# An encoder layer on one core: V projected in its own stretch and passed through DRAM, and one operand fewer fetched before the down phase

## The chip, the cores and the metric

The kernel runs on one core of a Trainium2 chip. The metric is the device time of one execution in microseconds (us). Before the change the median of three runs is 1965.58 us (1962.38 to 1968.96).

## The reference, cut to what matters

One layer of 1024 tokens and width 1024 in float32: a SwiGLU feed-forward block, a mixer of two attention kinds, and a second SwiGLU block, each followed by a residual sum and a layer norm. All of V comes out of the same product as Q and K, `p = h @ w_in`.

```python
def hybrid_mixer(h, w_in, w_out, ...):
    p = h @ w_in
    na_q, na_k, na_v, df_q, df_k, df_v = jnp.split(p, splits, axis=-1)
    na_out = neighbourhood_attention(na_q, na_k, na_v, na_rpb)   # 8 heads of 64, window 8 x 16
    df_out = differential_attention(df_q, df_k, df_v, ...)       # 4 heads, q and k of 2 x 64, v of 128
    return jnp.concatenate([na_out, df_out], axis=-1) @ w_out

x = layer_norm(a * x + 0.5 * swiglu(x, ffn1...))
x = layer_norm(a * x + hybrid_mixer(x, ...))
x = layer_norm(a * x + 0.5 * swiglu(x, ffn2...))
```

## The kernel before, in words

Each large product is made of three matmuls per term: both operands are split into a rounded part and a remainder (`split`: a cast on ScalarE, then a subtraction on VectorE or GpSimd), and hi x hi, hi x lo and lo x hi are added up in PSUM (`mm3`). A matmul is 128 x 128 against 128 x 512 columns wherever it can be.

The stages, in order: `gate_up` and `down_phase` of the first block, the attention, the product with w_out, `gate_up` and `down_phase` of the second block. All transfers are issued by the SP queue, in order. The order of the instructions on each engine is fixed when the program is built, by a scheduler that starts from the order of the code; the engines then run their lists in order and wait on semaphores.

**Attention.** There are eight groups: four differential heads (DF), then four pairs of neighbourhood heads (NA). `project(g)` makes K, V and Q of a group for both halves of the tokens, 24 matmuls for each of K, V and Q in each half. Its output has features as rows, so V has to be turned: `df_v` and `na_v` do it with transposes on TensorE (16 blocks of 128 x 128 per NA group, 8 per DF group), followed by copies. The projection of the first group runs alone. The other seven are fillers: `project` is a generator, cut into 48 pieces of three matmuls, and `Filler` places two pieces at each of 24 places of the attention of the group ahead. One DF group has eight units (blocks of 128 queries). A unit is: scores on TensorE, a sum with a minimum on VectorE (`df_scores`, L682), an exponential on ScalarE (L685), the reciprocal and the combination of the two maps on VectorE (L687 to L689), transposes of the result (L697), its split (L699, L700), and for every second unit the product with V (`df_out`, L706). An NA group has eight shorter units (`na_scores`, `na_transpose`, `na_out`); the last NA group has no filler.

**Down phase.** `fetch_down` loads a pair of operands (half of it activations from `hSd`, half weights), and splits it into a buffer of the pool `wsp` (4 buffers) or `hd`. `gate_up` fetches the operands 0 to 3 ahead, through the two staging buffers of the pool `wst`, which the last activations (`hPd`) also pass through. `down_phase` fetches the others through a pool of its own with six buffers.

Of the kernel before, what the change touches and what calls it, by code (L numbers as in the profile page):

```python
# [9 lines left out]
FT = mybir.dt.float32  # L10
# [11 lines left out]
P = 128  # L22
# [15 lines left out]
NA_R = [(0, 11), (4, 12)]  # L38
NA_C = [(0, 24, 0), (8, 32, 1), (24, 32, 1), (40, 24, 2)]
NA_KINDS = [(24, 0), (32, -8), (24, -8)]  # L40
NA_VOFF = [0, 16 * 24, 16 * 56, 16 * 88, 16 * 112]
RAW = 14 * NCOL + 32


# [1 line left out]
def tile_hybrid_layer(ctx: ExitStack, tc: tile.TileContext, I: dict, out: bass.AP, dbg=None):  # L46
# [22 lines left out]
    def split_w(src, pool=wsp, tag="wsp", eng=G):  # L69
        st = wst.tile([P, 1024], FT, name="wst")  # L70
        dma(st, src)
        sp = pool.tile([P, 2, 1024], FR, name=tag)
        split(sp[:, 0], sp[:, 1], st, eng)
        return sp
# [20 lines left out]
    x1d = dr.tile([8, P, DM], FT, name="x1d")  # L95
    x2d = dr.tile([8, P, DM], FT, name="x2d")
    oTd = dr.tile([8, P, S], FT, name="oTd")

    hPd = [dr.tile([4, P, S], FT, name=f"hPd{i}") for i in range(2)]
    hSd = [[dr.tile([P, 7, 512], FT, name=f"hSd{i}_{p}") for p in range(NP)] for i in range(2)]  # L100
# [107 lines left out]
    def gate_up(n, wgu, wd, W0=None, prelude=None):  # L208


        with ExitStack() as es:
# [152 lines left out]
            for f in range(2, NF):  # L364
# [37 lines left out]
                    sum_down(p)  # L402
                elif p + 1 < NP:
                    load_down(p + 1)
            down0.append(fetch_down(n, wd, 3, wst, wsp, "wsp"))
        return down0

    def down_phase(es, n, wd, down0, resid, g, b, post):
# [132 lines left out]
    def nothing():  # L541
        return
        yield

    with ExitStack() as es:
        kp = es.enter_context(tc.tile_pool(name="kp", bufs=2))
        qp = es.enter_context(tc.tile_pool(name="qp", bufs=3))
        vtp = es.enter_context(tc.tile_pool(name="vtp", bufs=1))
        sm = es.enter_context(tc.tile_pool(name="sm", bufs=6))
        mp = es.enter_context(tc.tile_pool(name="mp", bufs=1))  # L550
        rp = es.enter_context(tc.tile_pool(name="rp", bufs=2))
# [1 line left out]
        def project(g):  # L553

            h, na = g["h"], g["kind"] == "na"
            cq, ck, cv = (h, 4 + h, 8 + h) if na else (12 + h, 16 + h, 20 + h)
            scale = -0.125 if na else -0.125 / SLOPES[h]
            wk, wv, wq = (split_w(I["w_in"][c]) for c in (ck, cv, cq))
            K = g["K"] = kp.tile([P, 2, S], FR, name="K")
            VT = g["VT"] = vtp.tile([P, NA_VOFF[4] if na else S], FT, name="VT")  # L560
            g["Q"] = []

            def mm(w, t):
                ps = psB.tile([P, 512], FT, name="psB")
                for k in range(KT):
                    hi, lo = w[:, 0, k * P:(k + 1) * P], w[:, 1, k * P:(k + 1) * P]
                    xh, xl = xk(t, k)
                    T.matmul(ps, hi, xh, start=k == 0, stop=False)  # L568
                    T.matmul(ps, hi, xl, start=False, stop=False)  # L569
                    T.matmul(ps, lo, xh, start=False, stop=k == KT - 1)  # L570
                    if k < KT - 1:
                        yield ps
                yield ps

            for t in range(2):
                ts = slice(t * 512, (t + 1) * 512)
                for ps in mm(wk, t):
                    yield
                for j in range(2):
                    a, b = slice(64 * j, 64 * j + 64), slice(64 - 64 * j, 128 - 64 * j)  # L580
                    A.activation(K[a, j, ts], ps[a], AF.Copy, scale=scale)
                    V.scalar_tensor_tensor(K[b, j, ts], ps[a], scale, K[a, j, ts].bitcast(FT), OP.mult, OP.subtract)
                for ps in mm(wv, t):
                    yield
                if na:
                    psg = ps.rearrange("p (r c) -> p r c", c=GW)
                    for c, (c0, nc_, _) in enumerate(NA_C):
                        o = NA_VOFF[c] + 8 * t * nc_
                        A.copy(VT[:, o:o + 8 * nc_].rearrange("p (r c) -> p r c", c=nc_), psg[:, :, c0:c0 + nc_])
                else:  # L590
                    A.copy(VT[:, ts], ps)
                flush()
                Q = qp.tile([P, 2, 2, 512], FR, name="Q")
                g["Q"].append(Q)
                for ps in mm(wq, t):
                    yield
                for j in range(2):
                    a, b = slice(64 * j, 64 * j + 64), slice(64 - 64 * j, 128 - 64 * j)
                    qi, hi, lo = ps[a], Q[a, j, 0], Q[a, j, 1]
                    if na:  # L600
                        qi = qi.rearrange("p (r c w) -> p c r w", c=4, w=16)
                        hi, lo = (x.rearrange("p (c r w) -> p c r w", c=4, w=16) for x in (hi, lo))
                    A.copy(hi, qi)
                    V.tensor_tensor(lo, qi, hi.bitcast(FT), OP.subtract)
                    dma(Q[b, j].bitcast(FT), Q[a, j].bitcast(FT))

        PIECES = 48
        groups = [dict(kind="df", h=h) for h in range(4)] + [dict(kind="na", h=h) for h in range(4)]

        def filler(i, places):  # L610
# [35 lines left out]


        with ExitStack() as e2:
            vp = e2.enter_context(tc.tile_pool(name="vp", bufs=1))
            ep = e2.enter_context(tc.tile_pool(name="ep", bufs=3))  # L650
            ap = e2.enter_context(tc.tile_pool(name="ap", bufs=2))
            dp = e2.enter_context(tc.tile_pool(name="dp", bufs=1))
# [1 line left out]
            dist = dp.tile([P, 1920], FH, name="dist")  # L654
            dma(dist, I["dist"])

            def df_v(g):
                Vt = g["V"] = vp.tile([P, 2, KT, P], FR, name="Vt")
                for c in range(2):
                    ps = psB.tile([P, 4, P], FT, name="psB")  # L660
                    for k in range(4):
                        o = (4 * c + k) * P
                        T.transpose(ps[:, k], g["VT"][:, o:o + P], ident)
                    hi = Vt[:, 0, 4 * c:4 * c + 4]
                    A.copy(hi, ps)
                    V.tensor_tensor(Vt[:, 1, 4 * c:4 * c + 4], ps, hi.bitcast(FT), OP.subtract)

            def df_scores(g, qb):
                slope = SLOPES[g["h"]]
# [80 lines left out]
            for i, (g, qb) in enumerate(units):  # L750
                if qb == 0 and i:
                    fill.drain()
                    fill = filler(i // 8 + 1, 24)
                queue.append((g, qb, df_scores(g, qb)))
                if tail:
                    tail.pop()()
                fill()
                if qb == 1:
                    df_v(g)
                if len(queue) > 1:  # L760
                    df_rest()
            fill.drain()
# [10 lines left out]
        with ExitStack() as e2:  # L773
# [21 lines left out]
                        o += n * nc_  # L795

            def na_v(g, c):
                nc_ = NA_C[c][1]
                Vc = vp.tile([P, 4, P], FT, name="Vc")
                ps = psB.tile([P, 4, P], FT, name="psB")  # L800
                for k in range(4):
                    o = NA_VOFF[c] + 4 * k * nc_
                    T.transpose(ps[0:4 * nc_, k], g["VT"][:, o:o + 4 * nc_], ident)
                V.tensor_copy(Vc[0:4 * nc_], ps[0:4 * nc_])
                return Vc

            def na_scores(g, r, c, tabs):
# [157 lines left out]
def _layout(inp):  # L965
# [11 lines left out]
    for i in (1, 2):  # L977
        r[f"wgu{i}"] = gu(a[f"ffn{i}_w_gate"], a[f"ffn{i}_w_up"])
        r[f"wd{i}"] = a[f"ffn{i}_w_down"].reshape(NF, P, DM)
    r["w_in"] = np.ascontiguousarray(  # L980
        a["w_in"][0].reshape(KT, P, 24, P).transpose(2, 1, 0, 3)).reshape(24, P, KT * P)
    r["w_out"] = a["w_out"].reshape(8, P, DM)
    r["rpb"] = np.pad(a["na_rpb"].reshape(-1)[::-1], (RPB_PAD, RPB_PAD))
    for n in ("lq1", "lk1", "lq2", "lk2"):
# [36 lines left out]
```

## Time and profile before

| | before |
|---|---|
| median of three runs | 1965.58 us |
| profiled execution: its time / its span | 1969.43 us / 1967.7 us |
| TensorE (PE) busy | 1926.4 us, 98%, 9152 matmuls |
| VectorE (DVE) busy | 1217.6 us, 62% |
| ScalarE (ACT) busy | 762.3 us, 39% |
| GpSimd (POOL) busy | 208.8 us, 11% |
| mean granted TensorE clock | 0.993 |
| HBM read / written | 183.42 MB / 72.88 MB |

The span runs from the first to the last instruction; the time of the execution has some 2 us around it. Busy time of TensorE is the sum of the durations of pipelined matmuls, which overlap; how many matmuls a stretch really takes is read from their starts.

### The profile page before, as it was taken

The numbers are of one execution on the slowest core, as the hardware profiler recorded it, in microseconds if no ns is written. First come the engines' busy times: TensorE is split into PE (matmuls) and PEld (weight loads), VectorE is DVE, ScalarE is ACT, GpSimd is POOL, SyncE is SP. The second block draws the span as 40 slices with busy tenths as digits, with TensorE's granted clock in tenths as the row PEclk, the third lists the DMA queues.
The fourth block names the chain that finished last, engine by engine and source line by source line (L and its number), as shares of the span: only waits on it lengthen the run. The fifth ranks groups of instructions, "written<-read, shape, count | busy, mean of one in ns | idle before, by whom it ended". The sixth has DMA issues, their size and how long they took to land.

```text
span 1967.7 us, 24088 instructions
## 1 busy us (share of the span) xinstructions
PE 1926.4 (98%) x9152; PEld 1562.2 (79%) x9152; DVE 1217.6 (62%) x1823; ACT 762.3 (39%) x1228; POOL 208.8 (11%) x188
## 2 busy tenths in 40 slices
PE   9999999999999999999999999999999999999998
PEld 7777887877887878888777777887787888878887
DVE  8575655545555956778663346787666646455557
ACT  5333333334333245556544455133333333344331
POOL 0000000000001312011044443100000000000005
PEclk9999999999999999999999999999999999999999
DMA  4556323248762331112122226224555222387632
GB/s 168 208 203 222 120 102 118 102 166 300 235 196 88 106 91 41 49 41 62 30 56 67 64 65 226 83 89 160 192 205 191 93 102 99 125 294 254 195 119 86
DMA packets 90771, 266.26 MB, mean 135 GB/s; under 512 B 11680, under 2 KB 15648, under 8 KB 82976
## 3 DMA queue, kind: packets, MB, share of 16 engines
q1 hardware_dynamic: 90656, 264.73, 39.3%
q8 instruction: 72, 1.18, 0.2%
q14 instruction: 43, 0.35, 0.1%
HBM read 183.42 MB, written 72.88 MB: 130 GB/s over the span
## 4 chain that ended last, share of the span: by engine, by line
PE 42%; DMA 3%; DVE 3%; ACT 1%; issue 1%; POOL 0%; SPq 0%; POOLq 0%; DVEq 0%; ACTq 0%
PE psA L80 5%; PE psA L82 5%; PE psA L81 5%; PE psA L435 5%; PE psB L435 4%; PE psB L80 3%; PE psB L81 3%; PE psB L82 3%; PE psB L568 2%; PE psB L570 2%; PE psB L569 2%; PE psB L851 2%; PE psA L818 1%; DMA wr<-in_wgu 1%; PE psB L843 1%
## 5 line engine op out<-in xcount | busy, mean ns | idle before, releaser
L80 PE MATMUL psA<-x,wsp 128*128 128x512 f32 x448 | 181.5, 405 | 8.8 <-ACT t L377 5.3
L80 PE MATMUL psA<-s,wsp 128*128 128x512 f32 x480 | 189.6, 395 | 0.0
L82 PE MATMUL psA<-s,wsp 128*128 128x512 f32 x480 | 187.4, 390 | 0.0
L81 PE MATMUL psA<-s,wsp 128*128 128x512 f32 x480 | 186.7, 389 | 0.0
L66 ACT CAST wsp<-wr 128x1024 fp32r<-128x1024 f32 x124 | 128.9, 1049 | 128.9 <-DVE wr L205 121.3
L81 PE MATMUL psA<-x,wsp 128*128 128x512 f32 x448 | 175.8, 392 | 0.5 <-DVE x L67 0.5
L82 PE MATMUL psA<-x,wsp 128*128 128x512 f32 x448 | 175.1, 391 | 0.0
L568 PE MATMUL psB<-x,wsp 128*128 128x512 f32 x384 | 160.5, 418 | 0.0
L67 DVE TENSOR_TENSOR wsp<-wr,wsp 128x1024 fp32r<-128x1024 f32 x124 | 149.5, 1223 | 12.9 <-ACT wsp L66 12.9
L570 PE MATMUL psB<-x,wsp 128*128 128x512 f32 x384 | 152.2, 396 | 0.0
L569 PE MATMUL psB<-x,wsp 128*128 128x512 f32 x384 | 150.9, 393 | 0.0
L67 POOL TENSOR_TENSOR wsp<-wst,wsp 128x1024 fp32r<-128x1024 f32 x28 | 67.6, 2415 | 759.3 <-ACT wsp L66 759.3
L67 DVE TENSOR_TENSOR hd<-wst,hd 128x1024 fp32r<-128x1024 f32 x84 | 102.0, 1223 | 73.0 <-ACT hd L66 68.2
L204 DVE TENSOR_TENSOR wr<-wr 128x1024 f32<-128x1024 f32 x40 | 49.0, 1225 | 148.6 <-DMA wr<-in_wgu 148.6
L66 ACT CAST hd<-wst 128x1024 fp32r<-128x1024 f32 x84 | 87.7, 1054 | 124.7 <-PE psA L435 36.3
L66 ACT CAST wsp<-wst 128x1024 fp32r<-128x1024 f32 (+1 forms) x90 | 93.0, 1034 | 105.5 <-DMA wst<-in_wd 27.9
L67 DVE TENSOR_TENSOR wsp<-wst,wsp 128x1024 fp32r<-128x1024 f32 (+1 forms) x62 | 73.8, 1190 | 84.1 <-ACT wsp L66 76.0
L80 PEld LDWEIGHTS psA<-x,wsp 128*128 128x128 f32 x448 | 84.1, 188 | 45.4 <-ACT t L377 16.1
L435 PE MATMUL psA<-hd 128*128 128x512 f32 x504 | 116.2, 389 | 0.0
L144 POOL TENSOR_TENSOR mv<-mv,cols 128x1 f32<-128x1 f32 x24 | 35.5, 1478 | 721.1 <-DVE mv L143 721.1
L435 PEld LDWEIGHTS psA<-hd 128*128 128x128 f32 x504 | 94.6, 188 | 19.7
L80 PEld LDWEIGHTS psA<-s,wsp 128*128 128x128 f32 x480 | 90.0, 188 | 25.4 <-ACT sg L394 8.2
(183 smaller groups left out, 4096.4 us busy)
## 6 DMA issues: line engine op xcount, KB each, us to landing
wr<-in_wgu SPq DMA_DIRECT2D x42, 1024.0 KB, 4.8
hSd<-hs SPq DMA_DIRECT2D x18, 1792.0 KB, 5.7
wst<-hSd SPq DMA_DIRECT2D x126, 256.0 KB, 3.6
wst<-wTd SPq DMA_DIRECT2D x72, 256.0 KB, 3.7
wst<-in_wd SPq DMA_DIRECT2D x54, 256.0 KB, 4.8
wst<-in_w_in SPq DMA_DIRECT2D x24, 512.0 KB, 3.4
wt<-in_wd SPq DMA_DIRECT2D x18, 512.0 KB, 3.7
wt<-in_wd SPq DMA_DIRECT2D x36, 256.0 KB, 5.4
```

The costliest lines, as they stand in the source:

```text
L66: A.copy(hi, x)
L67: eng.tensor_tensor(lo, x, hi.bitcast(FT), OP.subtract)
L80: T.matmul(ps, ah, bh, start=start and j == 0, stop=False, skip_group_check=skip)
L81: T.matmul(ps, ah, bl, start=False, stop=False, skip_group_check=skip)
L82: T.matmul(ps, al, bh, start=False, stop=j == n - 1, skip_group_check=skip)
L144: G.tensor_tensor(mv[:, 3:4], mv[:, 2:3], mhalf[:, 0:1], OP.pow)
L204: V.tensor_tensor(l[:, 0:4:3], l[:, 2:4], l[:, 3:5], OP.subtract)
L435: T.matmul(banks[T_], o[:, x, a], o[:, w, 512:1024], start=start and p == 0 and j == 0, stop=p == NP - 1 and j == 2, skip_group_check=not ...
L568: T.matmul(ps, hi, xh, start=k == 0, stop=False)
L569: T.matmul(ps, hi, xl, start=False, stop=False)
L570: T.matmul(ps, lo, xh, start=False, stop=k == KT - 1)
L851: T.matmul(po[64 * j:64 * j + 64, c % 2], Vc[0:w, r + k, 64 * j:64 * j + 64], PTs[j][0:w, k], start=k == 0, stop=k == 2)
```

## The change

V of all heads is no longer part of `project`. A stretch of its own, between the first down phase and the attention, multiplies the transposed activations as the stationary operand with the columns of w_in for V, 512 at a time: 16 blocks (two kinds of heads, eight blocks of 128 tokens) of 24 matmuls. The output has tokens as rows. V of the DF heads is split and written to `vdd` in DRAM, V of the NA heads to `vnd`; `load_v` and `na_v` read them back for each group, with no transposes. `project` has 32 pieces instead of 48. Of the operands of the down phase, `gate_up` fetches 0 to 2 ahead, and number 3 is the first that `down_phase` fetches itself. The V pool of the DF groups gets two buffers.

```diff
+    vdd = dr.tile([P, 2, KT, 512], FT, name="vdd")
+    vnd = dr.tile([S, 512], FT, name="vnd")
...
                     load_down(p + 1)
-            down0.append(fetch_down(n, wd, 3, wst, wsp, "wsp"))
         return down0
...
+    with ExitStack() as es:
+        wv_p = es.enter_context(tc.tile_pool(name="wv", bufs=4))
+        dv = es.enter_context(tc.tile_pool(name="dv", bufs=2))
+        nv = es.enter_context(tc.tile_pool(name="nv", bufs=2))
+        wv = [[split_w(I["wv"][i, k], *((wv_p, "wv") if i else ())) for k in range(4)] for i in range(2)]
+        for i in range(2):
+            for tb in range(8):
+                o = slice(tb % 4 * P, tb % 4 * P + P)
+                ps = psB.tile([P, 512], FT, name="psB")
+                terms = []
+                for k in range(KT):
+                    w, cs = wv[i][k // 2], slice(k % 2 * 512, k % 2 * 512 + 512)
+                    hi, lo = xk(tb // 4, k)
+                    terms.append((hi[:, o], lo[:, o], w[:, 0, cs], w[:, 1, cs]))
+                mm3(ps, terms)
+                if tb:
+                    flush(1)
+                if i:
+                    v = nv.tile([P, 512], FT, name="nv")
+                    A.copy(v, ps)
+                    dma(vnd[tb * P:(tb + 1) * P], v)
+                else:
+                    v = dv.tile([P, 2, 512], FR, name="dv")
+                    split(v[:, 0], v[:, 1], ps, V)
+                    dma(vdd[:, :, tb], v.bitcast(FT))
...
-            wk, wv, wq = (split_w(I["w_in"][c]) for c in (ck, cv, cq))
+            wk, wq = (split_w(I["w_in"][c]) for c in (ck, cq))
...
-                for ps in mm(wv, t):
-                    yield
-                if na:
-                    psg = ps.rearrange("p (r c) -> p r c", c=GW)
-                    for c, (c0, nc_, _) in enumerate(NA_C):
-                        o = NA_VOFF[c] + 8 * t * nc_
-                        A.copy(VT[:, o:o + 8 * nc_].rearrange("p (r c) -> p r c", c=nc_), psg[:, :, c0:c0 + nc_])
-                else:
-                    A.copy(VT[:, ts], ps)
-                flush()
...
-        PIECES = 48
+        PIECES = 32
...
-            vp = e2.enter_context(tc.tile_pool(name="vp", bufs=1))
+            vp = e2.enter_context(tc.tile_pool(name="vp", bufs=2))
...
-            def df_v(g):
+            def load_v(g):
                 Vt = g["V"] = vp.tile([P, 2, KT, P], FR, name="Vt")
-                for c in range(2):
-                    ps = psB.tile([P, 4, P], FT, name="psB")
-                    for k in range(4):
-                        o = (4 * c + k) * P
-                        T.transpose(ps[:, k], g["VT"][:, o:o + P], ident)
-                    hi = Vt[:, 0, 4 * c:4 * c + 4]
-                    A.copy(hi, ps)
-                    V.tensor_tensor(Vt[:, 1, 4 * c:4 * c + 4], ps, hi.bitcast(FT), OP.subtract)
+                for i in range(2):
+                    dma(Vt[:, i].bitcast(FT), vdd[:, i, :, g["h"] * P:(g["h"] + 1) * P])
...
-                if qb == 1:
-                    df_v(g)
+                if qb == 0:
+                    load_v(g)
...
             def na_v(g, c):
-                nc_ = NA_C[c][1]
+                c0, nc_, _ = NA_C[c]
                 Vc = vp.tile([P, 4, P], FT, name="Vc")
-                ps = psB.tile([P, 4, P], FT, name="psB")
+                rows = vnd.rearrange("(r c) d -> r c d", c=GW)
                 for k in range(4):
-                    o = NA_VOFF[c] + 4 * k * nc_
-                    T.transpose(ps[0:4 * nc_, k], g["VT"][:, o:o + 4 * nc_], ident)
-                V.tensor_copy(Vc[0:4 * nc_], ps[0:4 * nc_])
+                    dma(Vc[0:4 * nc_, k], rows[4 * k:4 * k + 4, c0:c0 + nc_, g["h"] * P:(g["h"] + 1) * P])
                 return Vc
```

Three places of the instruction lists carry the argument. The first is the SP queue at the end of the first `gate_up`. In `hSd_3` the digit after the underscore is the number of the operand of the first product; `y` is the residual. Before, number 3 is loaded after the others, among the residual and the last `hPd` store:

```order
L192 DMA wst<-hSd_2_85 128x512
L193 DMA wst<-in_wd 128x512
L449 DMA y_2936<-in_x 128x1024
L192 DMA wst<-hSd_3_86 128x512
L237 DMA hPd_81<-wst 128x1024
L193 DMA wst<-in_wd 128x512
```

Now it follows at once on the store of the last `hSd`:

```order
L245 DMA hSd_8_93<-hs 128x3584
L193 DMA wst<-hSd_3_88 128x512
L194 DMA wst<-in_wd 128x512
L193 DMA wst<-hSd_4_89 128x512
L194 DMA wst<-in_wd 128x512
```

What moved: the loads of operand 3 stand first, and the pair 0 of the second product (`hSd_0` again) has moved back behind the residual.

The second is ScalarE from the end of the first down phase on. `x_75` and `x_76` are parts of the transposed activations, the last two pairs of them for the last two blocks of tokens. Before, the first group's projection follows:

```order
L66 CAST wsp<-wst 128x1024 x2
L164 CAST x_75<-psA 128x4x128
L164 CAST x_76<-psA 128x4x128
L591 COPY VT<-psB 128x512
L581 ACTIVATE K<-psB 64x512
L164 CAST x_75<-psA 128x4x128
L581 ACTIVATE K<-psB 64x512
L164 CAST x_76<-psA 128x4x128
```

Now the V stretch follows; `wv` are the weights for its second half, in memory that the down phase has just used, and `dv` its first blocks:

```order
L65 CAST wsp<-wst 128x1024 x2
L165 CAST x_75<-psA 128x4x128
L165 CAST x_76<-psA 128x4x128
L65 CAST wv<-wst 128x1024 x2
L65 CAST dv<-psB 128x512
L165 CAST x_75<-psA 128x4x128
L65 CAST dv<-psB 128x512
L165 CAST x_76<-psA 128x4x128
L65 CAST wv<-wst 128x1024 x2
L65 CAST dv<-psB 128x512 x5
```

What moved: the casts of `wv` stand ahead of the first two blocks of V and of the last block of activations.

The third is VectorE in the middle of the DF groups, one unit: the ISA rows are the sum with the minimum (two per unit) and the reading of its result, `rr` and `oT` belong to the output of the pair of units ahead, `aT` to the split of the unit ahead. Before:

```order
L720 TENSOR_SCALAR rr<-rr 128x2
L723 TENSOR_TENSOR rr<-rr,st 128x1 x2
L682 ISA e,st<-psA,dist 128x1024
L682 ISA st 128x1
L729 SCALAR_TENSOR_TENSOR oT<-o_sb,cols,psB 128x256
L684 TENSOR_SCALAR st<-st 128x1
L687 RECIPROCAL st<-st 128x2
```

Now:

```order
L729 TENSOR_SCALAR rr<-rr 128x2
L691 ISA e,st<-psA,dist 128x1024
L691 ISA st 128x1
L732 TENSOR_TENSOR rr<-rr,st 128x1 x2
L693 TENSOR_SCALAR st<-st 128x1 x2
L709 TENSOR_TENSOR aT<-psB,aT 128x4x128
L738 SCALAR_TENSOR_TENSOR oT<-o_sb,cols,psB 128x256
L709 TENSOR_TENSOR aT<-psB,aT 128x4x128
L691 ISA e,st<-psA,dist 128x1024
L691 ISA st 128x1
L696 RECIPROCAL st<-st 128x2
```

What moved: between the last TENSOR_SCALAR of a unit, which starts its exponential, and the reciprocal, which waits for that exponential, there was nothing; now two splits, an output and the next unit's sum stand there.

## Rows read from the trace of the kernel before

**Rows 1.** Windows: start:end length, PE, PEld, DVE, ACT, POOL busy (count), clock, DMA share, GB/s.

```profile
679.00:712.40 33.40, 33.40 (x154) 27.76 (x153) 12.25 (x18) 9.18 (x15) 10.50 (x5) 1.00 0.45 133
854.60:926.20 71.60, 70.71 (x394) 58.83 (x393) 54.44 (x115) 42.36 (x84) 9.96 (x7) 1.00 0.16 45
1057.80:1114.70 56.90, 56.77 (x338) 44.40 (x337) 20.92 (x68) 25.00 (x70) 25.84 (x33) 1.00 0.24 66
1175.20:1198.30 23.10, 22.24 (x150) 16.48 (x150) 15.21 (x54) 16.22 (x47) 11.49 (x14) 0.93 0.44 136
```

**Rows 2.** The chain that ended last: start us, us, engine, output, line, count.

```profile
986.57 0.87 PE psB L697 x8
...
1793.50 24.48 PE psA L435 x108
```

**Rows 3.** By line: the transposes of V (min/median/max ns), and a split of V.

```profile
L663 PE MATMUL psB<-ident,VT x32: 270/272/273, 719.2 to 941.0; 128*128 128x128 f32 x32
...
L803 PE MATMUL psB<-ident,VT x64: 270/272/421, 1011.0 to 1185.6; 128*96 128x128 f32 x32, 128*128 128x128 f32 x32
...
L666 DVE TENSOR_TENSOR Vt<-psB,Vt 128x512 fp32r<-128x512 f32 x8 | 5.2, 685 | 0.0
```

**Rows 4.** Timeline of VectorE: first sums of the DF groups 1, 2, 3.

```profile
784.68 1.21 DVE L682 CUSTOM_DVE_ANT_0 e<-psA,dist 128x1024 f32<-128x1024 f32 x1
...
854.64 1.22 DVE L682 CUSTOM_DVE_ANT_0 e<-psA,dist 128x1024 f32<-128x1024 f32 x1
...
926.22 1.22 DVE L682 CUSTOM_DVE_ANT_0 e<-psA,dist 128x1024 f32<-128x1024 f32 x1
```

**Rows 5.** Waits of VectorE in 854.6:926.2: total us, times, longest us.

```profile
DVE st L687 <- ACT e L685: 7.5, 6, 2.0
DVE rr L720 <- ACT oT L718: 3.1, 1, 3.1
DVE rr L723 <- POOL rr L721: 2.6, 3, 0.9
DVE K L582 <- ACT K L581: 1.9, 1, 1.9
DVE Q L604 <- ACT Q L603: 0.9, 1, 0.9
```

**Rows 6.** Timeline of VectorE: first sums of NA units (groups 1, 2; last group's first, last).

```profile
1057.77 0.43 DVE L822 CUSTOM_DVE_ANT_0 pe<-psA,tab 128x264 f32<-128x264 f32 x1 [0.34 <-PE psA L818]
...
1114.69 0.43 DVE L822 CUSTOM_DVE_ANT_0 pe<-psA,tab 128x264 f32<-128x264 f32 x1 [3.65 <-PE psA L818]
...
1175.17 0.41 DVE L822 CUSTOM_DVE_ANT_0 pe<-psA,tab 128x264 f32<-128x264 f32 x1
...
1198.35 0.45 DVE L822 CUSTOM_DVE_ANT_0 pe<-psA,tab 128x288 f32<-128x288 f32 x1
```

**Rows 7.** Timeline where the down phases begin: SP, ACT, PE; last, PE in the second.

```profile
451.93 0.42 SPq L193 DMA_DIRECT2D wst<-in_wd  x1
...
456.69 1.04 ACT L66 CAST wsp<-wst 128x1024 fp32r<-128x1024 f32 x1 [0.18 <-DMA wst<-in_wd]
...
457.79 0.80 PE L435 MATMUL psA<-wsp 128*128 128x512 f32 x1 [2.87 <-ACT wsp L66]
...
1750.60 1.00 PE L435 MATMUL psA<-wsp 128*128 128x512 f32 x2 [3.08 <-ACT wsp L66]
```

**Rows 8.** By line and form: the two halves of a weight split: busy us, mean ns.

```profile
L66 ACT CAST wsp<-wst 128x1024 fp32r<-128x1024 f32 x86 | 90.6, 1053 | 97.2 <-DMA wst<-in_wd 27.9 <-PE psB L435 22.4 <-PE psA L435 20.0
...
L67 POOL TENSOR_TENSOR wsp<-wst,wsp 128x1024 fp32r<-128x1024 f32 x28 | 67.6, 2415 | 759.3 <-ACT wsp L66 759.3
```

**Rows 9.** DMA issues: count, KB each, median us to landing.

```profile
wst<-in_w_in SPq DMA_DIRECT2D x24, 512.0 KB, 3.4
...
x1d<-y SPq DMA_DIRECT2D x8, 512.0 KB, 2.7
...
raw<-in_rpb SPq DMA_DIRECT2D x64, 29.1 KB, 1.9
```

More of the change, by code (lines that the diff above doesn't have):

```diff
@@ L40 @@
 NA_KINDS = [(24, 0), (32, -8), (24, -8)]
-NA_VOFF = [0, 16 * 24, 16 * 56, 16 * 88, 16 * 112]
 RAW = 14 * NCOL + 32
@@ L545, in tile_hybrid_layer @@
     with ExitStack() as es:
+        wv_p = es.enter_context(tc.tile_pool(name="wv", bufs=4))
[23 more added lines that the diff above has]
+    with ExitStack() as es:
         kp = es.enter_context(tc.tile_pool(name="kp", bufs=2))
         qp = es.enter_context(tc.tile_pool(name="qp", bufs=3))
-        vtp = es.enter_context(tc.tile_pool(name="vtp", bufs=1))
         sm = es.enter_context(tc.tile_pool(name="sm", bufs=6))
@@ L555, in project @@
             h, na = g["h"], g["kind"] == "na"
-            cq, ck, cv = (h, 4 + h, 8 + h) if na else (12 + h, 16 + h, 20 + h)
+            cq, ck = (h, 4 + h) if na else (12 + h, 16 + h)
             scale = -0.125 if na else -0.125 / SLOPES[h]
-            wk, wv, wq = (split_w(I["w_in"][c]) for c in (ck, cv, cq))
+            wk, wq = (split_w(I["w_in"][c]) for c in (ck, cq))
             K = g["K"] = kp.tile([P, 2, S], FR, name="K")
-            VT = g["VT"] = vtp.tile([P, NA_VOFF[4] if na else S], FT, name="VT")
             g["Q"] = []
@@ L981, in _layout @@
         a["w_in"][0].reshape(KT, P, 24, P).transpose(2, 1, 0, 3)).reshape(24, P, KT * P)
+    v = np.stack([np.split(a["w_in"][0], 6, axis=1)[i] for i in (5, 2)])
+    r["wv"] = np.ascontiguousarray(v.reshape(2, 4, 2, P, 512).transpose(0, 1, 3, 2, 4)).reshape(2, 4, P, 1024)
     r["w_out"] = a["w_out"].reshape(8, P, DM)
```

## The prediction

> **What bounds the kernel now.** I read three views in this order. The page's busy shares (in the table) say TensorE, 98%, so the first question is whether that engine is really full, and where. The chain that ended last gives the price of its work by starts: 108 matmuls of 512 columns take 24.48 us, 0.2267 each, and eight transposes 0.87 us, 0.109 each [rows 2]. The windows then show each stage of the attention with TensorE marked busy almost throughout, VectorE at 76% in a DF group (54.44 of 71.60) and at 37% in an NA group (20.92 of 56.90) [rows 1]. The mark is not to be trusted alone: in the last NA group, which has no filler, TensorE is busy for 22.24 of 23.10 us with only 150 matmuls [rows 1], and its units still follow each other much faster than in a group with fillers (3.31 us against 7.1, below). So I cost work on TensorE by starts, and ask in each stage what would set the pace if a third of the filler were gone.
>
> The V matmuls are 8 heads x 2 halves x 24 = 384 before, and 16 blocks x 24 = 384 after. Moving them costs or gives nothing by itself. What decides is whether the time they leave behind closes.
>
> **The change, part by part.**
>
> *The new stretch.* 384 x 0.2267 = +87.0 us. Its weights come as eight loads of 512 KB (3.4 us each [rows 9]) and eight splits, 1.05 us on ScalarE and 2.4 on GpSimd [rows 8]. The first two splits have their buffers early, the next two get theirs in the last microsecond or two of the down phase. Those two take until about 2 x 2.4 + 1.05 = 5.9 us after it, and TensorE has one block of transposes (0.9) and 18 matmuls (4.1) before it needs the last: a stall of about 1 us, between 0 and 3. ScalarE then waits in front of `wv` until the memory of the down phase is free, that is, until the last block's norm is stored and transposed. The transposes stand behind two blocks of V, 2 x 24 x 0.2267 = 10.9 us, and the store takes 2.7 [rows 9]: some 13 us. Queued behind it on ScalarE are the first two blocks of V and the last block of activations. TensorE waits for the first when it needs a fifth PSUM buffer, after four blocks or 21.8 us, and for the last after seven (38 us). So that wait is covered with some 8 us to spare, less the two casts of `wv`. VectorE has one split of 0.7 us per 5.4 us here. +1.0.
>
> *The first projection.* It runs alone, dense: 33.4 us [rows 1]. It loses 2 x 24 matmuls, -10.9.
>
> *DF groups.* They follow each other at 69.96 and 71.58 us [rows 4], 70.8 in the mean. TensorE loses 48 matmuls and 8 transposes per group (32 of them in all [rows 3]): 10.9 + 0.9 = 11.75, and 59.0 us remain if it goes on setting the pace with its small gaps as they are. That is one bound. The other is VectorE. In the second of these groups it waits 7.5 + 3.1 + 2.6 + 1.9 + 0.9 = 16.0 of 71.6 us [rows 5], so it is taken for 55.6, and 54.2 without the two splits of V (0.685 each [rows 3]). Of its waits, 7.5 are for the exponential of its own unit and 2.6 for GpSimd's power in the output; these belong to the unit and don't shrink when TensorE comes sooner. The other 5.9 are for ScalarE's copies of what the matmuls left, and do. With all of the first kind VectorE needs 54.2 + 10.1 = 64.3 us. The new list of VectorE puts two splits, an output and often the next sum between a unit's last small sum and its reciprocal, where there was nothing: that covers some of the 7.5. I take the middle of 59.0 and 64.3, 61.65: 9.15 less per group, four groups, -36.6. Bounds: -47 (59.0) and, if TensorE's lost work buys nothing but VectorE's 1.4 us per group, -5.6.
>
> *NA groups.* A group with 18 filler matmuls per unit takes 56.92 us for eight units, 7.11 each; the last group takes 23.18 for seven, 3.31 each [rows 6]. The difference, 3.80, is nearly the 18 x 0.2267 = 4.08 that the fillers cost: here fillers cover hardly anything. Six fewer per unit give 1.27 (their share of 3.80) to 1.36, for the 24 units of three groups 30.5 to 32.6. The 64 transposes of V are worth 64 x 0.109 = 7.0 [rows 2, 3], or nothing if other gaps hide them, since the units without fillers are not short of TensorE. I take -38.5, bounds -30.5 and -39.6.
>
> *V through DRAM.* SP gets 8 + 8 stores, 8 loads of 512 KB and 64 of 48 to 64 KB, each some 0.4 us on the queue ([rows 7] for a like one). Nearest landings: 2.7 us for a store of 512 KB, 3.4 for a load, 1.9 for small pieces [rows 9]. V of a DF group is wanted after the second unit, some 15 us after its load is issued; V of an NA unit three units later, 15 us or more. On SP they stand among loads of weights, of the position table `raw` and of Q, none due within a unit. Nothing, if that cover holds; if every NA group waited once for a landing it would be 4 x 2.
>
> *One operand fewer.* At the start of each down phase TensorE waits 2.87 and 3.08 us for operand 3. Its load goes out at 451.93, is cast at 456.69, and TensorE goes on at 457.79 [rows 7]. Now the load goes out first of all, into a buffer that waits for nothing in `wst`; the cast needs only the buffer of `wsp` that the last product of `gate_up` frees, while TensorE has operands 0 to 2 in between (36 matmuls or 8.2 us, part of them earlier). What is late next would be operand 9, which moves behind the residual; it is wanted six operands later, 6 x 12 x 0.2267 = 16 us. -6.0, and 0 if another wait takes over.
>
> *Sum:* 87.0 + 1.0 - 10.9 - 36.6 - 38.5 - 6.0 = -4.0 us. The profiled execution took 1969.4, so 1965.4 by it; the median of the runs is 3.85 lower, 1961.6. What a measurement of this kernel can tell from no change is about 0.3%, 5.9 us: the forecast is a small gain inside of that.
>
> **A rule against the change.** In a DF group TensorE and VectorE are both filled to three quarters or more, and V's matmuls, which ask nothing of VectorE there but two splits, fill TensorE while VectorE works [rows 1]. The Trainium skill's "Perfetto Trace Analysis", section Optimization Strategy, says that where the most-contended engine changes over time, interleaving the regimes may improve performance. By it the change goes the wrong way: it takes the regime of pure matmuls out. Followed to the end (the DF groups keep their pace but for 1.4 us) the sum would be -4.0 + 36.6 - 5.6 = +27; the NA rows, where the fillers are almost fully additive, speak against that for the other half.
>
> **Rivals.** *VectorE sets the pace in DF* (slower). All its waits stay and a group takes 64.3: -26.0 there, the sum is +6.6, 1972 us; the rule in full ends at +27, 1993. It turns into a loss that can be told at 64.1 us per group (2.5 x 4 = 9.9 more than forecast). For it: VectorE at 55.6 taken of 71.6 against 59.0 left for TensorE is close. Against it: its new list covers the wait for the exponential. *TensorE sets the pace everywhere* (faster): 87.0 - 10.9 - 47.0 - 39.6 - 6.0 = -16.5, 1949 us. For it: VectorE's taken time is still below TensorE's. Against it: two engines that wait for each other with like loads seldom both run full. *The down phases give nothing*: +2.0, 1968, no change. *The clock*: in the stretch without fillers, where TensorE ran 150 matmuls with gaps between them, the granted clock was 0.93 in the mean, that is the upper level of 2.4 GHz for all but a part of it, against 1.00 with fillers [rows 1]; at 0.93 through 24 NA units of 5.8 us at most 7% or 9.7 us would be lost: 1971, just inside of no change.
>
> **Chances.** No change that can be told (the forecast, and the two small rivals): 0.40. Faster by over 0.3%, TensorE setting the pace in most groups: 0.37. Slower by over 0.3%, 0.23: VectorE's waits 0.15, the rule in full 0.05, a wait at the head of the V stretch 0.03. Predicted time 1961.6. The range leaves out about 0.07 below 1950 (all of the faster rival) and 0.12 above 1977 (the DF groups beyond 65.5 us), and takes in 0 to 3 us at the stretch's head and the bounds of NA.
>
> **What would show it.** The V stretch: 87 to 90 us between the last transposes of the norm and the first projection, TensorE without waits above 3 us. The first sums of the DF groups 60 to 63 us apart, VectorE's wait for the exponential below 7.5 per group. NA units with fillers at 5.5 to 5.8 us. No wait of some 3 us for a cast at the head of the down phases. I am wrong if the DF groups stay above 64, or below 59.5, if TensorE waits for `Vt` or `Vc`, or if the wait at the head of the down phases only moves to another operand.

## The result and the profile after

The changed kernel takes 1952.51 us (median of five, 1949.34 to 1954.60) beside 1965.58 for the kernel before: ratio 0.9919, 95% interval 0.9902 to 0.9937, or 13 us faster. The forecast was 1961.6 and "no change that can be told" as the likeliest case. The time lies inside the range, but it is a gain that can be told, the case that had the second chance, and that case's reasons account for only a part of it.

The profiled execution took 1954.6 us. Page of the changed kernel:

```profile
span 1952.8 us, 24037 instructions
...
PE 1911.4 (98%) x9056; PEld 1549.9 (79%) x9056; DVE 1205.7 (62%) x1807; ACT 752.5 (39%) x1196; POOL 211.4 (11%) x188
```

96 matmuls (the transposes of V) and 15 us of busy time are gone, and TensorE is still at 98%: the page does not say where the 15 us came from. For that I laid the two traces beside each other by the starts of the same matmuls, in us from the span's start:

| matmul | before | after | difference | won or lost since the row above |
|---|---|---|---|---|
| first of the first down phase | 440.27 | 438.59 | -1.7 | -1.7 (scatter: 437.9 to 440.3 over the 14 traces) |
| its 61st | 466.36 | 458.07 | -8.3 | -6.6 |
| first transpose of the first norm | 638.24 | 626.72 | -11.5 | -3.2 |
| first behind the norm's next to last block | 679.00 | 665.91 | -13.1 | -1.6 |
| first score of DF | 712.65 | 775.76 | +63.1 | +76.2 (V's stretch 88.1, first projection -11.9) |
| first score of NA | 1003.41 | 1013.17 | +9.8 | -53.4 |
| last output of NA | 1206.37 | 1192.71 | -13.7 | -23.4 |
| first transpose of the second norm | 1244.56 | 1234.66 | -9.9 | +3.8 |
| first of the second down phase | 1727.34 | 1716.63 | -10.7 | -0.8 (scatter: 480.1 to 482.8 long in the 12 traces with this output product) |
| its 61st | 1757.98 | 1743.15 | -14.8 | -4.1 |
| end | 1967.60 | 1952.77 | -14.8 | 0 |

The attention as a whole (from row 4 to row 7), in which all the work on V lies, gives -0.6 us. The gain stands in two places outside of the work on V: the heads of the down phases (-6.6 and -4.1), and the tail of the first norm (-3.2 and -1.6).

The windows of the changed kernel that answer to [rows 1], with V's stretch first, then the first projection, a DF group, an NA group and 22 us of the last NA group:

```profile
665.90:754.00 88.10, 88.10 (x395) 72.94 (x394) 14.36 (x24) 20.74 (x30) 24.86 (x11) 1.00 0.51 169
754.00:775.80 21.80, 21.80 (x98) 18.06 (x97) 4.13 (x6) 5.06 (x8) 2.40 (x1) 1.00 0.33 83
836.60:897.20 60.60, 59.40 (x340) 49.37 (x339) 50.95 (x112) 39.72 (x79) 9.86 (x7) 1.00 0.27 73
1066.00:1111.80 45.80, 45.80 (x274) 34.58 (x274) 19.08 (x65) 22.52 (x62) 23.37 (x32) 1.00 0.35 93
1161.00:1183.00 22.00, 21.80 (x159) 16.89 (x161) 13.57 (x56) 17.29 (x52) 10.68 (x16) 0.92 0.39 121
```

VectorE's timeline, first sums of the DF groups [rows 4] and of two NA groups [rows 6]:

```profile
836.63 1.21 DVE L691 CUSTOM_DVE_ANT_0 e<-psA,dist 128x1024 f32<-128x1024 f32 x1
...
897.25 1.20 DVE L691 CUSTOM_DVE_ANT_0 e<-psA,dist 128x1024 f32<-128x1024 f32 x1
...
955.22 1.22 DVE L691 CUSTOM_DVE_ANT_0 e<-psA,dist 128x1024 f32<-128x1024 f32 x1
...
1066.65 0.43 DVE L829 CUSTOM_DVE_ANT_0 pe<-psA,tab 128x264 f32<-128x264 f32 x1 [0.46 <-PE psA L825]
...
1112.32 0.43 DVE L829 CUSTOM_DVE_ANT_0 pe<-psA,tab 128x264 f32<-128x264 f32 x1 [2.95 <-PE psA L825]
```

DF groups now follow each other at 60.6 and 58.0 us, 59.3 in the mean, where TensorE's own bound was 59.0 (and 59.5 the mark below which the forecast called itself wrong). All of VectorE's waits in the group from 836.6 to 897.2 [rows 5]:

```profile
DVE st L696 <- ACT e L694: 4.1, 5, 1.4
DVE e L691 <- PE psA L688: 3.4, 4, 1.4
DVE Q L619 <- ACT Q L618: 0.9, 1, 0.9
```

The wait for the exponential fell from 7.5 to 4.1 us, and VectorE now waits for TensorE's scores, which suggests that it does not set the pace (c1_dve below tests that).

### The profile page after: what moved, and what is told of

It is laid out like the page before. It is cut to its first block, busy times and chain, and to the rows that moved or that the text cites. A ratio compares the mean times of both kernels' runs of the same rounds, so it can differ in the third digit from the quotient of the medians.

```text
span 1952.8 us, 24037 instructions
## 1 busy us (share of the span) xinstructions
PE 1911.4 (98%) x9056; PEld 1549.9 (79%) x9056; DVE 1205.7 (62%) x1807; ACT 752.5 (39%) x1196; POOL 211.4 (11%) x188
## 5 line engine op out<-in xcount | busy, mean ns | idle before, releaser
L66 POOL TENSOR_TENSOR wsp<-wst,wsp 128x1024 fp32r<-128x1024 f32 x24 | 60.8, 2538 | 774.2 <-ACT wsp L65 774.2
L65 ACT CAST wsp<-wst 128x1024 fp32r<-128x1024 f32 (+1 forms) x86 | 88.7, 1032 | 97.7 <-DMA wst<-wTd 20.7
L79 PEld LDWEIGHTS psA<-s,wsp 128*128 128x128 f32 x480 | 90.0, 188 | 25.4 <-ACT sg L395 8.2
L593 PE MATMUL psB<-x,wsp 128*128 128x512 f32 x256 | 107.1, 418 | 0.0
L81 PEld LDWEIGHTS psA<-s,wsp 128*128 128x128 f32 x480 | 90.1, 188 | 19.7
L80 PEld LDWEIGHTS psA<-s,wsp 128*128 128x128 f32 x480 | 90.2, 188 | 17.9
```

Source lines behind the costliest of these rows:

```text
L65: A.copy(hi, x)
L66: eng.tensor_tensor(lo, x, hi.bitcast(FT), OP.subtract)
L79: T.matmul(ps, ah, bh, start=start and j == 0, stop=False, skip_group_check=skip)
L80: T.matmul(ps, ah, bl, start=False, stop=False, skip_group_check=skip)
L81: T.matmul(ps, al, bh, start=False, stop=j == n - 1, skip_group_check=skip)
```

## The experiments

**Theory A:** the gain is made by the operand that is fetched later (its wait costs about twice its length, through the clock) and by the lambda work, which no longer stands in the norm's tail; V's stretch is worth nothing. **Rival B:** the operand gives its 6 us of waits, as forecast, and V's stretch the other 7. Ratios are to the kernel before, timed on the same chip, with a 95% interval; us are made of them with a time before of 1967.

What A rests on. Windows of the kernel before, around the first head:

```profile
450.00:455.00 5.00, 4.92 (x21) 3.49 (x19) 3.73 (x4) 3.33 (x4) 0.00 (x0) 1.00 0.89 292
455.00:460.00 5.00, 2.21 (x5) 1.57 (x6) 5.00 (x6) 3.51 (x4) 0.00 (x0) 0.72 0.99 367
460.00:465.00 5.00, 5.00 (x15) 3.86 (x15) 2.02 (x2) 2.04 (x2) 0.00 (x0) 0.59 1.02 385
465.00:470.00 5.00, 5.00 (x24) 4.12 (x23) 4.54 (x4) 3.23 (x4) 0.00 (x0) 1.00 1.06 389
```

In the slice after the wait of 2.87 us TensorE is "busy" for 5.00 of 5.00 us and starts 15 matmuls, not 24: the granted clock is 0.59 in the mean, the lower of the two levels (1.2 GHz) for most of the slice. And VectorE's timeline in the first norm of the kernel before:

```profile
629.76 0.69 DVE L131 SCALAR_TENSOR_TENSOR y<-y,psB 128x512 f32<-128x512 f32 x1 [1.30 <-PE psB L82]
633.81 0.29 DVE L622 TENSOR_TENSOR wst<-wst 128x128 f32<-128x128 f32 x1 [3.36 <-DMA wst<-in_lk]
634.02 0.69 DVE L133 BATCH_NORM_STATS2 st<-y 128x6 f32<-128x512 f32 x1
...
636.90 1.28 DVE L153 SCALAR_TENSOR_TENSOR y<-y,mv,gb 128x1024 f32<-128x1024 f32 x1
```

and TensorE's:

```profile
638.24 1.97 PE L161 MATMUL psA<-ident,y 128*128 128x128 f32 x8 [3.07 <-DVE y L153]
```

L622 is the first product of the lambda work, 0.29 us long, which has nothing to do with the norm. It waits for its load, the norm's statistics (L133) stand behind it, and TensorE waits behind the norm. The clock falls here too: it is 0.66 in the mean from 638 to 643 us, and of the 4.8 us that this tail is longer than in the changed kernel, 3.07 are the wait and the other 1.7 stand in those slow matmuls. In the changed kernel the scheduler puts L622 behind V's splits, so it is no part of the norm.

**One edit alone, and both, without V.**

```diff
--- e1_operand (and in e4_both)
-            down0.append(fetch_down(n, wd, 3, wst, wsp, "wsp"))
--- e3_lam (and in e4_both)
-        lt = wst.tile([P, 1024], FT, name="wst")
+        lt = mp.tile([P, 386], FT, name="lt")
--- e2_v: after, with the fetch of operand 3 put back
+            down0.append(fetch_down(n, wd, 3, wst, wsp, "wsp"))
```

> The kernel before with one edit of the change alone: operand 3 of the down phases is no longer fetched at the end of the gate and up products. Theory A (the wait of 2.87 and 3.08 us costs again as much, because the granted clock falls behind it: the two heads of the down phases came 6.15 and 5.18 us sooner after the change): 11.3 us faster than before, 1954.3 us, granted clock 1.00 in the 15 us after each head, where it was 0.72 and 0.59 in two slices of 5 us. Rival B (the forecast's own term, only the waits are saved and V gave the rest): 6.0 us faster, 1959.6 us. A third outcome, 0, would say that the wait moves to another operand.

Measured: 0.9964 (0.9951 to 0.9977), -7.1 us: the interval, -9.6 to -4.5, holds B's 6.0 and leaves out A's 11.3, so the time alone speaks for B. In its trace, though, both heads are shorter by what A says (the first 61 matmuls take 6.3 us less at the first, 5.0 at the second), and the clock stays up:

```profile
455.00:460.00 5.00, 5.00 (x24) 4.14 (x23) 3.18 (x3) 1.19 (x2) 0.00 (x0) 1.00 0.99 352
460.00:465.00 5.00, 5.00 (x24) 4.14 (x23) 3.04 (x3) 3.47 (x4) 0.00 (x0) 1.00 1.06 398
```

but 2.9 us of it are lost again in the last NA group (below), and 1.8 at the output product.

> The kernel before with the lambda work (four loads of 64 numbers, one product, one reduction, one exponential) in memory of its own that comes free only after the first norm, in place of a buffer of the weights' ring; nothing else is changed. Theory A: the wait of 3.4 us for its load in the list of VectorE in the middle of the first norm, and the 3.07 us that TensorE waits behind it, are gone: 4.8 us faster than before, 1960.8 us. Rival B: the norm's tail was shortened by V's stretch and not by the lambda work: 0, 1965.6 us.

Measured: 0.9977 (0.9968 to 0.9987), -4.5 us; the norm's tail is 4.8 us shorter in the trace, VectorE without the wait:

```profile
627.61 0.69 DVE L131 SCALAR_TENSOR_TENSOR y<-y,psB 128x512 f32<-128x512 f32 x1 [1.30 <-PE psB L82]
628.33 0.69 DVE L133 BATCH_NORM_STATS2 st<-y 128x6 f32<-128x512 f32 x1
```

> The kernel before with both small edits (operand 3 not fetched ahead, the lambda work in memory of its own) and V as it was. Theory A: 16.1 us faster than before, 1949.5 us, so 3 us faster than the whole change: V's stretch through DRAM adds nothing to it. Rival B: 6.0 us faster than before, 1959.6 us, 7 us slower than the whole change.

Measured: 0.9922 (0.9907 to 0.9936), -15.3 us, as A has it. The two small edits alone give what the whole change gives.

> The kernel after the change with operand 3 fetched ahead again, so that V's stretch stands alone. Theory A: 11.3 us slower than after, 1.8 us faster than before, 1963.8 us: V's own stretch costs in its 88.1 us what the other groups save (-0.6 over the whole attention), 3.8 us are lost at the head of the output product, and 4.8 us are saved in the tail of the first norm where the lambda work no longer stands. Rival B: 6.0 us slower than after, 1958.5 us.

Measured: 0.9983 (0.9971 to 0.9994), -3.3 us. V's stretch and the lambda work that it displaces together give no more than the lambda work alone (e3_lam, -4.5). B falls.

**The changed kernel again, and the output product cut otherwise.**

> The changed kernel unaltered, timed beside the next kernels on one chip. Theory A (V's stretch adds nothing beside the two small edits): 0.992 of before, the same as the kernel with the two small edits alone. Rival B (V's stretch is worth some 7 us): a ratio below that kernel's by 0.003 or more.

Measured: 0.9924 (0.9907 to 0.9941). Operand 3 can now be read from three pairs: 7.1 us (e1_operand), 10.8 (e4_both beside e3_lam), 11.6 (this beside e2_v); lambda from two: 4.5 (e3_lam) and 8.3 (e4_both beside e1_operand). The second and third figure for operand 3 lie clear of the forecast's 6.0, the first does not; a_again and e2_v ran on two chips, each beside its own runs of the kernel before.

```diff
--- b1_after_wout (on after), b2_small_wout (on e4_both)
-        m.down(hs[0:2], wo[0:2], ALPHA)
-        m.down(hs[2:8], wo[2:8], 1.0, post2)
+        m.down(hs[0:4], wo[0:4], ALPHA)
+        m.down(hs[4:8], wo[4:8], 1.0, post2)
```

> The kernel after the change with the output product cut 4 + 4 in place of 2 + 6 of its eight operands, so that its first pass (43.5 us of matmuls in place of 21.8) covers the loads of the residual and of the last four heads. Theory A (the 3.8 us lost at its head are these loads): 3 to 5 us faster than the changed kernel, ratio about 0.990 of before. Rival: the loss at the head is scatter of single executions, and the time stays at that of the changed kernel.

Measured: 0.9922 (0.9903 to 0.9941), nothing. TensorE's waits in the output product, first of the changed kernel (1192 to 1298 us):

```profile
PE psB L79 <- DVE y L132: 2.9, 2, 1.5
```

among VectorE's waits there (1185 to 1216 us), the one for the residual:

```profile
DVE y L132 <- DMA y<-x1d: 2.0, 2, 1.2
```

then TensorE's with the new cut:

```profile
PE psA L162 <- DVE y L154: 1.8, 1, 1.8
```

The wait at the head is gone, so it was for the loads, of the residual `x1d` above all; a new one stands at the tail. That the second pass, now shorter per block, no longer covers a norm there is argued from that row, not tested. It has moved, not shrunk by anything the time can tell.

> The kernel before with the two small edits (operand 3, lambda) and the same cut of the output product, V as it was before. Theory A: V adds nothing, so the same as the changed kernel with that cut, within 3 us; since the kernel with the two small edits lost nothing at that head in its profile, 0 to 3 us faster than without the cut, ratio 0.990 to 0.992 of before. Rival B (V's stretch is worth some 7 us): 7 us slower than the changed kernel with that cut.

Measured: 0.9945 (0.9927 to 0.9962), 4.5 us slower than b1_after_wout; between A and B, and by itself it decides nothing.

**The clock behind the wait.**

```diff
--- e7_warm, in product() of down_phase, before's kernel
+                if k == 2:
+                    ps = psB.tile([P, 512], FT, name="psB")
+                    for _ in range(12):
+                        T.matmul(ps, o[:, 0, 0:P], o[:, 0, 512:1024], start=True, stop=True)
```

> The kernel before with 12 matmuls more, whose result nobody reads, right ahead of operand 3's first in each down phase: 12 x 0.2267 = 2.7 us, about the wait that is there. Theory A (of the 6.3 and 5.1 us that the two heads lose, 3.3 and 1.8 are the matmuls after the wait, 0.43 us apart in place of 0.2267, because the granted clock fell to its lower level in the wait): these matmuls run at 0.2267 again, 5.1 us faster than before. Rival (the matmuls after the wait are far apart because their own operands come late): no gain, 0 to 1 us slower.

Measured: 0.9997 (0.9985 to 1.0008), no gain. Its trace shows the mechanism all the same (TensorE's timeline; before, the two matmuls of operand 3 and the four behind them took 2.8 us from the first start to that of the next):

```profile
452.98 2.88 PE L440 MATMUL psB<-wsp 128*128 128x512 f32 x12
456.15 0.73 PE L435 MATMUL psA<-wsp 128*128 128x512 f32 x2 [0.29 <-DMA y<-in_x]
457.10 1.19 PE L435 MATMUL psB<-hd 128*128 128x512 f32 x4 [0.21 <-ACT hd L66]
458.12 2.43 PE L435 MATMUL psA<-wsp 128*128 128x512 f32 x10
```

and the windows of the same stretch:

```profile
455.00:460.00 5.00, 4.50 (x19) 3.10 (x18) 3.98 (x4) 2.00 (x2) 0.00 (x0) 1.00 1.01 397
460.00:465.00 5.00, 5.00 (x24) 4.14 (x23) 3.18 (x3) 3.47 (x4) 0.00 (x0) 1.00 1.05 394
```

The ten matmuls at 458.12 take 2.43 us where they were 0.43 apart, with no other operands: the half speed was the clock's. The heads, from the 36th matmul to the 61st, are 2.4 and 1.2 us shorter in this trace, 3.6 in place of 5.1; 2.7 are lost in its last NA group. The times do not bear the gain out: their interval, 3.0 us faster to 1.6 slower, leaves 3.6 out. What the fallen clock costs is thus shown in traces, and not by the times of this run.

**What sets the pace of the DF groups.**

```diff
--- c1_dve, in df_scores of after
+                t = ep.tile([P, 512], FT, name="t", bufs=1)
+                V.tensor_copy(t, e[1][:, 0:512])
                 V.reciprocal(rz, z)
```

> The changed kernel with one more copy of 128x512 numbers on VectorE in each of the 32 DF units, whose result nobody reads: by the nearest rows at most 0.69 us each, 22 us in all, 5.5 per DF group. VectorE waits 8.4 and 7.5 us in the two groups looked at. Theory A (TensorE sets the pace of the DF groups at 59 us): 0 to 8 us slower. Rival C (the forecast's other bound, VectorE sets the pace): 15 to 22 us slower.

Measured: 0.9942 (0.9929 to 0.9956), 4 us slower than the changed kernel. Groups by line, its copies between 780 and 1000 us:

```profile
L697 DVE COPY t<-e 128x512 f32<-128x512 f32 x29 | 13.3, 458 | 0.8 <-ACT e L694 0.7
```

32 x 0.458 = 14.7 us more on VectorE cost 4 us, uncertain by some 4, and the DF part of the trace (first score of DF to first of NA) is 2.9 us longer, 240.3 for 237.4. That is A's range and far from C's: TensorE sets the pace.

**Work for the idle places.** To see whether TensorE's idle time can be had, the last pieces of the NA filler were held back for the group that has none, and the first NA tables shared between two engines, on both kernels.

```diff
--- b3_hold (on after); with the tables: b4_hold_tab (on after), b5_small_hold_tab (on e4_both)
-                if i > 4:
+                if 4 < i < 7:
                     fill = filler(i + 1, 24)
+                if i == 6:
+                    fill.rate = 25.1 / 24
                 for r in range(2):
+                    if i == 7 and r == 1:
+                        fill.drain()
...
-                fill.drain()
+                if i != 6:
+                    fill.drain()
--- the tables
-            def na_tables(g, r, E=G):
+            def na_tables(g, r, E=(G, G)):
-                        E.tensor_tensor(tab[:, os_]
+                        E[j].tensor_tensor(tab[:, os_]
-            na_tables(groups[4], 0, V)
+            na_tables(groups[4], 0, (V, G))
```

(In b5_small_hold_tab the rate is 41.1 / 24, for its 48 pieces.)

> The changed kernel with the last 7 pieces of the filler (21 matmuls of the last NA head's second half of Q, which only its last four units read) held back out of the sixth group into the last NA group, which has no filler and starts with a wait of TensorE of 2.4 us and a granted clock of 0.91. Theory A (TensorE sets the pace and what it loses is lost where it stands idle): the third NA group is 21 x 0.2267 = 4.8 us shorter, the last one takes them into gaps that are 17.8 us in all, and its clock goes to 1.00: 3 to 6 us faster than the changed kernel, ratio 0.989 to 0.991 of before. Rival (in the last group these matmuls are simply added): 0, ratio 0.992.

Measured: 0.9901 (0.9885 to 0.9916), 4 us faster than the changed kernel, as A has it, though the two intervals overlap and the changed kernel was not timed beside it. In its trace the NA groups together take 175.0 us in place of 179.5; the last one grows from 35.2 to 36.3 and its clock is 0.95, not the 1.00 of A.

> The same, and the first tables of the NA groups (six additions, 5.28 us on VectorE in one piece, while TensorE waits 2.9 us for the sums behind them and then runs 10 us at a granted clock of 0.66) shared between VectorE and GpSimd. Theory A: that wait falls below 1 us and the clock stays near 1.00 there: another 3 to 5 us, ratio 0.986 to 0.989 of before. Rival (GpSimd needs as long for its half as VectorE for the whole, or the wait is the memory's, which comes free late): 0, as without.

Measured: 0.9899 (0.9884 to 0.9913): nothing more in the times. Windows of the changed kernel: the third NA group, the last one, and the 10 us behind the tables:

```profile
1111.80:1157.50 45.70, 44.64 (x273) 33.88 (x272) 22.37 (x69) 25.32 (x67) 19.91 (x32) 1.00 0.35 98
1157.50:1192.70 35.20, 30.52 (x226) 23.16 (x225) 20.47 (x68) 22.83 (x65) 18.97 (x21) 0.91 0.46 146
1035.00:1045.00 10.00, 9.25 (x43) 7.23 (x43) 6.17 (x26) 7.27 (x22) 4.81 (x9) 0.66 0.33 68
```

and of b4_hold_tab:

```profile
1111.60:1151.70 40.10, 40.10 (x253) 30.49 (x253) 19.56 (x65) 22.44 (x62) 20.41 (x30) 1.00 0.34 86
1151.70:1186.50 34.80, 32.54 (x246) 24.10 (x245) 21.45 (x71) 25.35 (x70) 19.48 (x21) 1.00 0.51 167
1037.00:1047.00 10.00, 7.59 (x46) 5.44 (x46) 4.38 (x19) 5.16 (x17) 7.47 (x13) 1.00 0.23 63
```

The third group gives up 5.6 us, and the last one takes the 20 matmuls more without growing. Behind the tables the clock is at 1.00, but TensorE now waits there, for up to 2.6 us, for GpSimd, which has its share of the tables ahead of the units' work.

> The kernel before with the two small edits and with both of the last two edits (the filler's last pieces held back, the tables shared), V as it was before. Theory A (V's stretch of its own is worth nothing): the same time as the changed kernel with both, within 3 us. Rival B (V's stretch is worth some 7 us): 7 us slower than that.

Measured: 0.9884 (0.9868 to 0.9899), 1944.8 us, the fastest of all, without V's stretch. What V's stretch is worth, from four pairs with and without it: +1.2 us (e2_v, e3_lam), +0.4 (a_again, e4_both), -4.5 (b1, b2), +3.0 (b4, b5); in the mean 0; each is uncertain by 3 to 5 us, so a worth of 2 or 3 us either way is not excluded.

## Why the prediction was wrong

**The step that failed** is "One operand fewer": -6.0, the two waits of 2.87 and 3.08 us and nothing else [rows 7]. The granted clock falls during such a wait and stays down behind it, so a wait of 3 us cost 6.3 us at the first head and 5.0 at the second (trace of e1_operand). The trace of before held this, in windows of 5 us over the heads; the clock was read in the attention only. The term measures -11.3 in that trace, -7.1 to -11.6 in the times; the lowest of these does not tell it from the forecast's 6.0, and e7_warm, which kept the clock up, gained nothing that the times show. That the term was too small is shown by two pairs of three; that the clock is why, by the traces.

**A term was missing.** The lambda work in the norm's tail (4.8 us in the trace, 4.5 in the times) is in neither list of what the change moves: the diff does not touch it. It moves because V's weights come ahead of it in the ring `wst` (the order shows that; that it is the ring was only argued). The wait of 3.36 us for `in_lk` stood in the trace of before; I had no row of the norm's tail. From the forecast's -4.0 to the -14.8 us between the two traces, then: the heads -4.7 (-10.7 for -6.0), the lambda work -4.8, V -2.6, the head of the output product +3.8, scatter in stretches that the change does not shorten -2.5.

**The V part** was right in its sum, 88.0 - 10.9 - 75.1 = +2.0 against -0.6, out of two errors that nearly cancel, which is luck. DF gives 11.4 per group (the first sums of groups 0 to 3 are 178.0 us apart in place of 212.2), so -45.5 for four in place of -36.6: TensorE's bound, not the middle. Taking the middle between an engine at 59.0 and one at 64.3 had no row behind it, and neither had the argument that two engines with like loads seldom both run full. Of the 10.1 us of waits that were to stay on VectorE, 4.1 are left in the group shown; c1_dve shows what slack that leaves. The NA groups and the tail of DF give the rest, -76.8 + 45.5 = -31.3 in place of -38.5: the two full groups 11.2 each (57.0 to 45.8), DF's tail 7.9, but the first group only 1, and the last nothing (35.3 to 35.2), at a clock of 0.91 in place of 0.95. The first loses only 18 matmuls, 292 to 274, where a full group loses some 63: before, the others of its filler were run in DF's tail. The sum is near the bound of -30.5, in which the transposes of V buy nothing, but not for that reason: a full group gives more than the 10.9 that its 48 matmuls cost, so there the transposes bought a little; what is short is the first group and the last. **V through DRAM** cost nothing there, as forecast: no wait of TensorE for `Vt` or `Vc`. But the attention ends while the loads of the output product are not done, and 3.8 us go back at its head (1.9 in a_again).

**The stretch itself** came out at 88.1 us against 88.0, but not for the reason given: the 1.0 us of stall did not occur (TensorE waits nowhere in it). In its place stand the transposes of the norm's last block, which before stood in the first projection; that one gave 11.9 in place of 10.9 for the same reason. The two shifts cancel.

**The rule against the change.** The Trainium skill's "Perfetto Trace Analysis", section Optimization Strategy, says that where the most-contended engine changes over time, interleaving the regimes may improve performance. Taking V's matmuls out of the DF groups brought no loss here: these took 59.3 us, not the 69.4 of the rule followed to its end. Nor was taking the pure matmuls out a gain. By c1_dve TensorE sets the pace in the DF groups as it does in V's stretch, so that the condition of the rule was not met.

The rival "TensorE sets the pace everywhere" came nearest (1949): right for DF, wrong for NA, and short of the two terms above.

## What to carry to other kernels

Price a wait of TensorE of some 3 us together with the granted clock in the slices behind it: in the traces here such a wait cost 4.8 to 6.3 us. When a change moves loads in a ring or a queue, go through everything that a scheduler may move with them, and look for small instructions with a load of their own in the list of a busy engine. V's matmuls, which TensorE does at full pace in either place, cost the same here wherever they stood; what gave time was to take a wait of TensorE away or, as far as the noise lets one say (b3_hold), to fill its idle places.

## What the hardware showed that was not expected

Kernels with one and the same order of instructions on their engines in the last NA group ran it at two paces. Windows of the group, and of 10 us about its longest wait, e3_lam:

```profile
1164.00:1202.40 38.40, 33.75 (x242) 25.66 (x240) 20.59 (x72) 23.57 (x67) 17.98 (x21) 0.91 0.44 139
1174.00:1184.00 10.00, 8.22 (x48) 6.71 (x49) 5.43 (x22) 6.07 (x21) 5.18 (x7) 0.66 0.29 107
```

and e4_both:

```profile
1158.70:1193.30 34.60, 31.50 (x242) 23.44 (x240) 22.88 (x72) 23.29 (x67) 17.55 (x21) 1.00 0.49 155
1158.00:1168.00 10.00, 7.97 (x58) 6.02 (x57) 7.53 (x17) 6.30 (x16) 5.04 (x5) 1.00 0.38 107
```

The number of matmuls is the same, 242; the granted clock and 3.8 us are not. ScalarE's timeline at that place, e3_lam:

```profile
1172.13 1.04 ACT L66 CAST wsp<-wst 128x1024 fp32r<-128x1024 f32 x1 [4.21 <-DMA wst<-in_w_out]
...
1174.17 0.61 ACT L844 COPY PT<-psB 96x256 f32<-96x256 f32 x2
```

and e4_both:

```profile
1165.53 1.04 ACT L66 CAST wsp<-wst 128x1024 fp32r<-128x1024 f32 x1 [0.62 <-DMA wst<-in_w_out]
```

In the one a cast of an output weight waits 4.21 us for its load, with the copies that TensorE needs behind it; TensorE waits 2.8 us for them and the clock falls. In the other the cast waits 0.62, TensorE waits 1.9 us elsewhere, for VectorE, and the clock stays. Of the six traces with this NA code three show 38 us (e1_operand, e3_lam, e7_warm, each with that wait of some 4 us) and three 34.6 to 35.3 (before, e4_both, b2_small_wout). The six traces show where they part. At the start of the group two splits run at the same time, one on VectorE and one on GpSimd. e3_lam:

```profile
1164.56 0.69 DVE L67 TENSOR_TENSOR x<-wst,x 128x512 fp32r<-128x512 f32 x1 [3.17 <-ACT x L66]
1164.66 2.82 POOL L67 TENSOR_TENSOR wsp<-wst,wsp 128x1024 fp32r<-128x1024 f32 x1
```

and e4_both:

```profile
1159.57 2.66 DVE L67 TENSOR_TENSOR x<-wst,x 128x512 fp32r<-128x512 f32 x1 [3.52 <-ACT x L66]
1159.32 2.37 POOL L67 TENSOR_TENSOR wsp<-wst,wsp 128x1024 fp32r<-128x1024 f32 x1
```

In the three traces of 38 us VectorE starts 0.10 to 0.24 us ahead and takes 0.69 to 0.84 us, GpSimd 2.82 to 2.83. In the three others VectorE starts between 0.07 us ahead and 0.26 behind and takes 2.66 to 2.97, GpSimd 2.36 to 2.37: one of the two is held up, and some 0.1 us decide which. GpSimd's end frees the buffer for the load, which so goes out some 3.5 us after the group's start in the first three and 3.0 in the others; where VectorE is held up, ScalarE comes to the cast 2.3 us later and finds the load nearly done. This is read from six traces; no run forced the one order or the other. The difference is as large as several of the effects looked for here, and may be one reason why a single trace and the median over executions differ by some us.
